# A streaming encoder layer in fp32: the first group's square moves to SBUF and GpSimd, and h comes back in one load for the final sum

## The chip, the cores and the metric

The kernel runs on one core of one Trainium2 chip. The metric is the device time of one execution in microseconds (us), as the median of several runs. The engines are called PE (TensorE), DVE (VectorE), ACT (ScalarE), POOL (GpSimd) and SP (SyncE, which issues most of the DMAs).

## What is computed

One layer of an encoder is computed in fp32 for 1024 prompt frames and 32 sample frames (whose 512 past frames lie in a cache). The model's width is 1024, the width of the feed-forward part (FFN) 4096. Two attention mixers and two gates come first; what matters here is the end of the layer:

```python
def merge_and_ffn(x, o_a, o_b, gate_a, gate_b, w_branch_a, w_branch_b, w_out, g_ffn, w_up, w_down):
    B, L = x.shape[:2]
    pa = jnp.einsum('blc,cd->bld', o_a.reshape(B, L, WIDTH_A), w_branch_a)
    pb = jnp.einsum('blc,cd->bld', o_b.reshape(B, L, WIDTH_B), w_branch_b)
    m = jax.nn.sigmoid(gate_a) * pa + jax.nn.sigmoid(gate_b) * pb
    h = x + jnp.einsum('bld,de->ble', m, w_out)
    u = jnp.einsum('bld,df->blf', rmsnorm(h, g_ffn), w_up)
    return h + jnp.einsum('blf,fd->bld', jnp.square(jax.nn.relu(u)), w_down)
```

`rmsnorm(h, g)` is h * rsqrt(mean(h^2) + eps) * g. Its factor per frame is the same for all features, so the kernel takes it out: the FFN runs on h * g, and because the square doubles the power, its result is multiplied at the end by `rb2` = 1 / (mean(h^2) + eps).

## The kernel before

**Layout and products.** Activations lie feature-major: 128 features on the partitions, frames along the free axis. Every fp32 product is made of three passes in the faster format fp32r. Each operand is split into a rounded high part and the rest, and `three` adds high x high, high x rest and rest x high into one PSUM bank. In the rows, `wh` and `wl` are the parts of a weight, `xh` and `xl` those of an activation. `unit` (L435) brings a weight of 128x512 on chip: SP loads it into `wst` (3 buffers), ScalarE casts it to `wh`, GpSimd subtracts to get `wl` (5 buffers each). So each weight that PE multiplies costs GpSimd one subtraction.

**Banks.** `column_block` (L474) takes a PSUM bank (`bank`, L426), issues the matmuls of one output tile and then calls `done`, which reads the bank. The bank is free for another tile when the last instruction that reads or writes it has ended.

**Order.** The kernel's instructions are first recorded, then put in order by a planner (`Plan`) that simulates the engines with estimated costs. Where several instructions could go next on an engine, a rank decides: FAST, then PREP (loads and weight splits), MAIN, FILL (matmuls of a column block), SLOW. Nothing is reordered on the chip: each engine runs its list in order and waits on semaphores. Since the planner issues everything, every row of the profile has the same line, L410 (`fn(*args, **kw)`), and groups are told apart by tile names.

**The two groups.** After the attention of the first frames, the end of the layer (gates, `w_out`, FFN) runs for two groups of columns. Group 0 has columns 0 to 511 in one chunk of 512. It runs beside the attention that is still left (generators called by `beside`), and attention holds six of the eight banks: the group has two, tagged `pj`. Its h * g lies in `g.h` and `g.l`, which are the tiles xh[0] and xl[0] (xh_92 and xl_93 in the rows); the squares lie in `g.mh` and `g.ml`, in xh[1] and xl[1] (xh_94, xl_95). Group 1 has columns 512 to 1055 in two chunks of 272, tiles gh and gl of its own, and all banks: six `pj` for the up-projection, two `pd` for the down-projection. Its up-projection makes two by two blocks of outputs with seven products in place of eight (`go_up_quad`), whose weight sums are formed by loads that add in flight. `hv`, the sum h of the layer's middle, is also written to DRAM (`dh`), because g.h holds it only multiplied by g and rounded.

**The FFN** (`ffn_group`, L1436). d_ff is cut in eight quarters of 512, as the code calls them. In group 0, `go_up(f)` (L1453) makes 128 features of u with 24 matmuls and two weights, and hands the bank to `square` (L1427): ScalarE writes relu to an SBUF tile `ru`, VectorE multiplies the bank by it in place (`scalar_tensor_tensor`, pj<-pj,ru in the rows), ScalarE casts the bank to `uh`, VectorE subtracts to get `ul` (the row `xl<-pj,xh`). The bank is held through all four. In group 1 the same function squares the quad's outputs, one of each pair with sign -1.

`go_down(e, q)` (L1506) multiplies the four feature blocks of quarter q with the weight for output block e (12 matmuls a chunk) and adds the bank to `g.y`: in quarter 0 ScalarE copies it, later VectorE adds, and in the last quarter VectorE multiplies the bank by rb2, adds y and SP stores the sum. So that this sum is already h + rb2 * (all others), the kernel in quarter 6 (nq - 2), behind each down-projection, loads h of this block from `dh` into a tile `hx` (tag sg, 3 buffers), and GpSimd multiplies y by rb2 and adds hx.

Per quarter, group 0 runs four up-projections (the first of them ahead of the quarter), then eight down-projections; in the last quarter two down-projections of quarter 6 (KEEP, e = 6 and 7) come between. Group 1 alternates a quad of the next quarter with four down-projections of this one. `rb2` is `g.acc`, and appears as acc in the rows.

Of the kernel before, what the change touches and what calls it, by code (L numbers as in the profile page):

```python
# [9 lines left out]
F32 = mybir.dt.float32  # L10
# [10 lines left out]
KB = D // 128  # L21
# [31 lines left out]
FAST, PREP, MAIN, FILL, SLOW = 0, 1, 2, 3, 4  # L53
# [365 lines left out]
class Layer:  # L419
# [1007 lines left out]
    def square(self, g, ps, uh, ul, sign=1.0):  # L1427

        nc = self.nc
        r = g.tmp("ru", "pb", 3)  # L1430
        nc.scalar.activation(r, ps, AF.Relu, scale=sign)
        nc.vector.scalar_tensor_tensor(ps, ps, sign, r, op0=ALU.mult, op1=ALU.mult)
        nc.scalar.copy(uh, ps)
        nc.vector.tensor_sub(ul, ps, uh.bitcast(F32))

    def ffn_group(self, g, late=iter(())):  # L1436
        nc, a, i = self.nc, self.a, g.i
        n = g.n
        rb2 = g.acc

        def scales():

            for c in range(len(g.chunks)):
                ps = self.bank("pj")
                nc.tensor.matmul(ps[:, :n], self.ones, g.acc[c], start=True, stop=True)
                with nc.rank(FAST):
                    v = g.tmp("rv", "pb", 3)
                    nc.vector.tensor_scalar(v, ps[:, :n], 1.0 / D, EPS, op0=ALU.mult, op1=ALU.add)
                    nc.vector.reciprocal(rb2[c], v)

        nq, us = DFF // 512, {}

        def go_up(f):  # L1453
            units = [self.unit(a["w_up"][f, j]) for j in range(2)]
            us[f] = uh, ul = g.mh[:, f % 8], g.ml[:, f % 8]
            self.column_block(units, lambda k, cs: (g.h[:, k, cs], g.l[:, k, cs]),
                              lambda c, cs, ps: self.square(g, ps, uh[:, cs], ul[:, cs]), g.chunks)

        def go_up_quad(f):

            a11, a12, a22, s1, s2, s3, s4 = self.quad_units(f)
            for i in range(2):
                us[f + i] = g.mh[:, (f + i) % 8], g.ml[:, (f + i) % 8]
            ta, tb, tc, td = ([(th[:, k], tl[:, k]) for k in range(4)] for th, tl in g.sums)
            x = lambda j, c: [(g.h[:, 4 * j + k, c * n:c * n + n], g.l[:, 4 * j + k, c * n:c * n + n]) for k in range(4)]

            def product(w, xs, ps=None):
                first = ps is None
                if first:
                    ps = self.bank("pj")[:, :n]  # L1470
                with nc.rank(FILL):
                    for k in range(4):
                        ks = slice(k * 128, k * 128 + 128)
                        self.three(ps, w[0][:, ks], w[1][:, ks], *xs[k], first and k == 0, k == 3, skip_group_check=True)
                return ps

            def keep(ps):
                t = nc.tile(self.op, [128, g.w], F32, "part", tag="o32", bufs=4)[:, :n]
                with nc.rank(FAST):
                    nc.scalar.copy(t, ps)  # L1480
                return t

            def done(i, c, out, ps, more=None):
                cs = slice(c * n, c * n + n)
                uh, ul = us[f + i]
                with nc.rank(FAST):
                    if more is not None:
                        nc.vector.tensor_add(out, ps, more)
                    self.square(g, out, uh[:, cs], ul[:, cs], -1.0 if i else 1.0)

            px = product(a11, x(0, 0))
            p1 = keep(px)
            pz = product(s1, ta)
            p5 = keep(pz)
            product(s2, tb, px)
            u2 = keep(px)
            product(s4, x(1, 1), pz)
            done(0, 1, pz, pz, u2)
            py = product(a12, x(1, 0))
            done(0, 0, py, py, p1)  # L1500
            product(s3, tc, px)
            done(1, 1, self.bank("pj")[:, :n], px, p5)
            product(a22, td, px)
            done(1, 0, px, px)

        def go_down(e, q):  # L1506
            units = [self.unit(a["w_down"][e, q])]

            def done(c, cs, ps):
                y = g.y[:, e, cs]  # L1510
                if q == 0:
                    nc.scalar.copy(y, ps)
                elif q < nq - 1:
                    nc.vector.tensor_add(y, ps, y)
                else:
                    nc.vector.tensor_mul(ps, ps, rb2[c])
                    nc.vector.tensor_add(y, ps, y)
                    nc.sync.dma_start(self.o["yT"][:, e, slice(g.lo + cs.start, g.lo + cs.stop)], y)

            self.column_block(units, lambda k, cs: (us[4 * q + k][0][:, cs], us[4 * q + k][1][:, cs]), done, g.chunks,  # L1520
                              kn=4, tag="pd" if g.i else "pj")
            if q == nq - 2:
                for c, cs in enumerate(g.chunks):
                    y = g.y[:, e, cs]
                    with nc.rank(PREP):
                        hx = nc.tile(self.op, [128, g.w], F32, "hx", tag="sg", bufs=3)[:, :n]
                        nc.sync.dma_start(hx, self.dh[e, :, slice(g.lo + cs.start, g.lo + cs.stop)])
                        nc.gpsimd.tensor_mul(y, y, rb2[c])
                        nc.gpsimd.tensor_add(y, y, hx)

        done = 0

        def beside(n):

            nonlocal done
            done += n
            while done >= PACE:
                done -= PACE
                nc.patience = WAIT[2]
                with nc.behind():  # L1540
                    next(late, None)
                nc.patience = WAIT[1]

        if g.i:
            go_up_quad(0)
            scales()
            go_up_quad(2)
            for q in range(nq):
                for i in range(2):
                    if q < nq - 1:  # L1550
                        go_up_quad(4 * q + 4 + 2 * i)
                    for e in range(4 * i, 4 * i + 4):
                        go_down(e, q)
            return
        go_up(0)
        scales()
        for q in range(nq):
            for f in range(4 * q + 1, min(4 * q + 5, 4 * nq)):
                go_up(f)
                beside(2)  # L1560
            if q == nq - 1:
                for e in KEEP:
                    go_down(e, q - 1)
            for e in range(KB):
                if q != nq - 2 or e not in KEEP:
                    go_down(e, q)
                beside(1)
# [81 lines left out]
```

## Time and profile before

| | |
|---|---|
| median of three runs | 1787.98 us (1787.19 to 1790.59) |
| profiled execution | 1787.43 us, its span 1785.7 us |
| mean granted TensorE clock | 0.998 of full speed |
| instructions | 32620, of them 11394 matmuls |
| traffic of the span | 264.5 MB, 148 GB/s on average |

Six stretches of the span, as busy us of each engine (the windows view):

| us of the span | what runs | PE | DVE | ACT | POOL | DMA share |
|---|---|---|---|---|---|---|
| 0 to 460 (460 us) | input projections, first attention | 450.3 | 353.8 | 296.2 | 179.9 | 0.46 |
| 460 to 850 (390) | attention, gates and w_out of group 0 | 383.2 | 253.0 | 243.5 | 278.4 | 0.63 |
| 850 to 1127 (277) | FFN of group 0 beside late attention | 272.1 | 162.2 | 156.7 | 136.2 | 0.42 |
| 1127 to 1310 (183) | FFN of group 0 alone | 179.0 | 51.1 | 63.8 | 113.9 | 0.44 |
| 1310 to 1430 (120) | gates and w_out of group 1 | 115.6 | 82.0 | 66.7 | 99.8 | 0.74 |
| 1430 to 1786 (356) | FFN of group 1 | 346.5 | 147.6 | 150.8 | 218.8 | 0.61 |

A row of the profile reads: line, engine, operation, output tile <- input tiles, partitions x elements and type. A group has a count (x32), its busy us, the mean ns of one, and behind the second bar the idle time that lay ahead of its instructions on that engine with what ended most of it. A timeline row has the start in us, the duration, the instruction, and in brackets the idle time just ahead of it and who ended it.

### The profile page before, as it was taken

Reading aid. Unit: us, or ns where it says so; the run is one execution under the profiler, and the core shown is the slowest. Engines: PE = TensorE matmul, PEld = TensorE weight load, DVE = VectorE, ACT = ScalarE, POOL = GpSimd, SP = SyncE. Lnnn points to the kernel's source line nnn. Section 1 sums busy time; section 2 is a strip of 40 time slices with the busy share of each in tenths; the row PEclk is TensorE's granted clock in tenths of the full one; section 3 lists DMA queues with packets and bytes.
Section 4 is the critical chain, followed back from the end, with each engine's and each line's share of the span. In section 5 each row is a group of like instructions: output and inputs, shape, how many; then the busy total and the mean of one; then the engine's idle time right before and its main releaser. Section 6 shows DMA issues by size and latency. Waiting matters only on the chain.

```text
span 1785.7 us, 32620 instructions
## 1 busy us (share of the span) xinstructions
PE 1746.7 (98%) x11394; PEld 1601.3 (90%) x11394; DVE 1049.7 (59%) x2304; ACT 977.7 (55%) x2153; POOL 1026.9 (58%) x901
## 2 busy tenths in 40 slices
PE   8999999999999999999999999999999999999998
PEld 7999999999899888988888888888799999999998
DVE  7555678999566645888755555222247843444434
ACT  7444599973256766666665456533236654444441
POOL 3623332435276675998664444644859966666675
PEclk9999999999999999999999999999999999999999
DMA  7244451544665667566344443533487676666633
GB/s 258 71 130 121 116 172 58 161 144 132 201 174 158 169 199 209 169 177 180 104 139 114 123 139 101 155 94 95 130 256 197 162 172 151 152 151 154 153 78 108
DMA packets 171283, 264.53 MB, mean 148 GB/s; under 512 B 29296, under 2 KB 60624, under 8 KB 171120
## 3 DMA queue, kind: packets, MB, share of 16 engines
q1 hardware_dynamic: 161472, 245.33, 47.4%
q0 software_dynamic: 9216, 16.78, 6.0%
q8 instruction: 90, 1.47, 0.3%
q14 instruction: 73, 0.60, 0.1%
q10 hardware_dynamic: 432, 0.34, 0.1%
HBM read 207.87 MB, written 54.40 MB: 147 GB/s over the span
## 4 chain that ended last, share of the span: by engine, by line
PE 83%; DMA 5%; POOL 4%; DVE 4%; issue 2%; ACT 1%; SPq 0%; ACTq 0%; POOLq 0%; DVEq 0%
PE pj L410 51%; PE s L410 13%; PE pd L410 10%; PE t L410 5%; PE o L410 4%; POOL wl L410 2%; DMA sg<-dg 1%; DVE xl L410 1%; DMA raw<-w_up 1%; POOL y L410 1%; DMA q<-dq 1%; POOL xl L410 1%; POOL acc L410 1%; POOL pb L410 0%; SPq L410 0%
## 5 line engine op out<-in xcount | busy, mean ns | idle before, releaser
L410 POOL TENSOR_TENSOR wl<-wst,wh 128x512 fp32r<-128x512 f32 x350 | 483.4, 1389 | 390.4 <-ACT wh L410 365.4
L410 PE MATMUL pj<-xh,wh 128*128 128x512 f32 (+1 forms) x1600 | 558.3, 350 | 7.0 <-DVE y L410 4.0
L410 PE MATMUL pj<-xh,wl 128*128 128x512 f32 (+1 forms) x1600 | 558.2, 350 | 0.7 <-POOL wl L410 0.7
L410 PE MATMUL pj<-xl,wh 128*128 128x512 f32 (+1 forms) x1600 | 556.6, 348 | 0.1
L410 ACT CAST wh<-wst 128x512 fp32r<-128x512 f32 x350 | 216.4, 620 | 328.8 <-PE pj L410 181.1
L410 PEld LDWEIGHTS pj<-xh,wh 128*128 128x128 f32 x1600 | 301.0, 188 | 43.5 <-DVE y L410 5.2
L410 PEld LDWEIGHTS pj<-xh,wl 128*128 128x128 f32 x1600 | 301.1, 188 | 34.2 <-POOL wl L410 1.2
L410 PEld LDWEIGHTS pj<-xl,wh 128*128 128x128 f32 x1600 | 301.3, 188 | 32.3 <-DVE xl L410 0.6
L410 PE MATMUL pd<-xh,wl 128*128 128x272 f32 x512 | 148.0, 290 | 3.3 <-POOL wl L410 3.3
L410 PE MATMUL pd<-xh,wh 128*128 128x272 f32 x512 | 148.1, 289 | 1.9 <-ACT y L410 1.6
L410 PE MATMUL pd<-xl,wh 128*128 128x272 f32 x512 | 148.0, 289 | 0.0
L410 DVE TENSOR_TENSOR tt<-t,tt 128x512 fp32r<-128x512 f32 (+2 forms) x168 | 100.3, 622 | 49.4 <-ACT tt L410 47.5
L410 DVE TENSOR_TENSOR_SCAN rem<-rem 128x896 f32<-128x896 f32 (+6 forms) x66 | 121.6, 1865 | 12.3 <-ACT rem L410 12.1
L410 ACT ACTIVATE junk<-score,cand 128x384 bf16<-128x384 f32 (+1 forms) x124 | 116.0, 936 | 9.4 <-DVE cand L410 7.3
L410 POOL TENSOR_TENSOR p<-p,rem 128x895 f32<-128x895 f32 (+6 forms) x66 | 99.2, 1516 | 32.2 <-DVE rem L410 29.8
L410 ACT CAST tt<-t 128x512 fp32r<-128x512 f32 (+2 forms) x168 | 84.7, 541 | 44.3 <-PE t L410 40.3
L410 PEld LDWEIGHTS o<-tt,v 128*128 128x128 f32 x640 | 92.6, 188 | 11.3 <-ACT wh L410 1.5
L410 PE MATMUL s<-wl,xh 128*128 128x256 f32 (+1 forms) x360 | 101.8, 286 | 0.2 <-POOL wl L410 0.2
L410 PE MATMUL s<-wh,xh 128*128 128x256 f32 (+1 forms) x360 | 100.3, 286 | 0.9 <-DVE small L410 0.7
L410 PE MATMUL s<-k,q 128*128 128x384 f32 (+5 forms) x384 | 95.7, 357 | 5.4 <-DMA k<-dk 2.3
L410 PE MATMUL s<-wh,xl 128*128 128x256 f32 (+1 forms) x360 | 100.8, 283 | 0.0
L410 PE MATMUL o<-tt,v 128*128 128x256 f32 (+1 forms) x640 | 99.0, 278 | 1.4 <-DVE o L410 0.7
(252 smaller groups left out, 3829.0 us busy)
## 6 DMA issues: line engine op xcount, KB each, us to landing
wst<-w_down SPq DMA_DIRECT2D x128, 256.0 KB, 2.7
raw<-w_up SPq DMA_DIRECT2D x80, 256.0 KB, 3.1
q<-dq SPq DMA_DIRECT2D x64, 256.0 KB, 5.3
wst<-w_up SPq DMA_DIRECT2D x64, 256.0 KB, 2.7
raw<-w_up POOLq DMA_DIRECT2D x64, 256.0 KB, 4.5
k<-dk SPq DMA_DIRECT2D x48, 256.0 KB, 3.9
v<-dv SPq DMA_DIRECT2D x48, 256.0 KB, 3.9
wst<-w_g SPq DMA_DIRECT2D x42, 256.0 KB, 3.4
```

What stands on the lines that cost most here:

```text
L410: fn(*args, **kw)
```

## The change

Two parts of the FFN are written in another way.

*The square of group 0.* The relu goes to the SBUF tile `ru` as before. GpSimd then squares that tile in place, ScalarE casts it to `uh`, and VectorE subtracts `uh` from it. The bank is read by the relu alone. Group 1's square stays as it is.

*The final sum, in both groups.* The `hx` tiles and their loads (8 in group 0, 16 in group 1) are gone. When the last up-projection is through, nothing reads `g.h` any more, and one DMA (`reload`, ranked PREP) brings all of h from `dh` into it: 128x8x512 fp32 in group 0, 128x8x544 in group 1. The sum of a block is made in two ways, in the last quarter. For e from 4 to 7 GpSimd multiplies y by rb2 and adds h, now recorded just ahead of the block's last matmuls (rank MAIN instead of PREP); VectorE then does as before. For e from 0 to 3 GpSimd does nothing: VectorE adds y to the bank, multiplies the bank by rb2 and writes bank + h to y. Each block is stored as before.

```diff
--- before.py
+++ after.py
@@ -1429,6 +1429,11 @@
         nc = self.nc
         r = g.tmp("ru", "pb", 3)
         nc.scalar.activation(r, ps, AF.Relu, scale=sign)
+        if not g.i:
+            nc.gpsimd.tensor_mul(r, r, r)
+            nc.scalar.copy(uh, r)
+            nc.vector.tensor_sub(ul, r, uh.bitcast(F32))
+            return
         nc.vector.scalar_tensor_tensor(ps, ps, sign, r, op0=ALU.mult, op1=ALU.mult)
         nc.scalar.copy(uh, ps)
         nc.vector.tensor_sub(ul, ps, uh.bitcast(F32))
@@ -1510,23 +1515,33 @@
                 y = g.y[:, e, cs]
                 if q == 0:
                     nc.scalar.copy(y, ps)
-                elif q < nq - 1:
+                    return
+                if q < nq - 1:
                     nc.vector.tensor_add(y, ps, y)
-                else:
-                    nc.vector.tensor_mul(ps, ps, rb2[c])
-                    nc.vector.tensor_add(y, ps, y)
-                    nc.sync.dma_start(self.o["yT"][:, e, slice(g.lo + cs.start, g.lo + cs.stop)], y)
-
+                    return
+                if e < KB // 2:
+                    nc.vector.tensor_add(ps, ps, y)
+                    y = hx_of(e, cs)
+                nc.vector.tensor_mul(ps, ps, rb2[c])
+                nc.vector.tensor_add(g.y[:, e, cs], ps, y)
+                nc.sync.dma_start(self.o["yT"][:, e, slice(g.lo + cs.start, g.lo + cs.stop)], g.y[:, e, cs])
+
+            if q == nq - 1 and e >= KB // 2:
+                for c, cs in enumerate(g.chunks):
+                    y = g.y[:, e, cs]
+                    nc.gpsimd.tensor_mul(y, y, rb2[c])
+                    nc.gpsimd.tensor_add(y, y, hx_of(e, cs))
             self.column_block(units, lambda k, cs: (us[4 * q + k][0][:, cs], us[4 * q + k][1][:, cs]), done, g.chunks,
                               kn=4, tag="pd" if g.i else "pj")
-            if q == nq - 2:
-                for c, cs in enumerate(g.chunks):
-                    y = g.y[:, e, cs]
-                    with nc.rank(PREP):
-                        hx = nc.tile(self.op, [128, g.w], F32, "hx", tag="sg", bufs=3)[:, :n]
-                        nc.sync.dma_start(hx, self.dh[e, :, slice(g.lo + cs.start, g.lo + cs.stop)])
-                        nc.gpsimd.tensor_mul(y, y, rb2[c])
-                        nc.gpsimd.tensor_add(y, y, hx)
+
+        def hx_of(e, cs):
+
+            return g.h.bitcast(F32)[:, e, cs]
+
+        def reload():
+
+            with nc.rank(PREP):
+                nc.sync.dma_start(g.h.bitcast(F32), self.dh[:, :, g.lo:g.lo + g.w].rearrange("e p t -> p e t"))
 
         done = 0
 
@@ -1546,6 +1561,8 @@
             scales()
             go_up_quad(2)
             for q in range(nq):
+                if q == nq - 1:
+                    reload()
                 for i in range(2):
                     if q < nq - 1:
                         go_up_quad(4 * q + 4 + 2 * i)
@@ -1559,6 +1576,7 @@
                 go_up(f)
                 beside(2)
             if q == nq - 1:
+                reload()
                 for e in KEEP:
                     go_down(e, q - 1)
             for e in range(KB):
```

## The prediction

> **What bounds the kernel now.** I read the page first.
>
> ```profile
> span 1785.7 us, 32620 instructions
> PE 1746.7 (98%) x11394; PEld 1601.3 (90%) x11394; DVE 1049.7 (59%) x2304; ACT 977.7 (55%) x2153; POOL 1026.9 (58%) x901
> ```
>
> TensorE is busy for 98% of the span, and the change neither adds nor removes a matmul. All that it can win is in the 39 us in which PE stands still, so the next view is the table of who PE waited for, cut to 740 to 1300 us, where the first group's FFN runs.
>
> ```profile
> PE pj L410 <- DVE y L410: 4.0, 5, 0.9
> PE pj L410 <- ACT y L410: 1.7, 1, 1.7
> ...
> PE pj L410 <- DVE xl L410: 0.8, 2, 0.6
> PE pj L410 <- POOL wl L410: 0.7, 1, 0.7
> ```
>
> The columns are total us, times and longest. Five waits of 0.8 us that look alike come once per quarter of the FFN, so one of them is followed in the timeline (start, duration, engine, operation; in brackets the idle time before it).
>
> ```profile
> 1244.90 0.59 ACT L410 ACTIVATE ru<-pj 128x512 f32<-128x512 f32 x1
> 1245.52 0.70 DVE L410 SCALAR_TENSOR_TENSOR pj<-pj,ru 128x512 f32<-128x512 f32 x1 [3.40 <-ACT ru L410]
> 1246.25 0.59 ACT L410 CAST xh<-pj 128x512 fp32r<-128x512 f32 x1 [0.77 <-DVE pj L410]
> 1246.85 0.39 PE L410 MATMUL pj<-xh,wl 128*128 128x512 f32 x1
> 1247.27 0.69 DVE L410 TENSOR_TENSOR y<-pj,y 128x512 f32<-128x512 f32 x1 [1.05 <-PE pj L410]
> 1247.88 0.68 DVE L410 TENSOR_TENSOR xl<-pj,xh 128x512 fp32r<-128x512 f32 x1
> 1248.02 0.50 PE L410 MATMUL pj<-xh,wh 128*128 128x512 f32 x1 [0.78 <-DVE y L410]
> 1248.36 0.40 PE L410 MATMUL pj<-xl,wh 128*128 128x512 f32 x1
> ```
>
> The group has two PSUM banks. The last up-projection of the quarter holds one from its relu at 1244.90 until `xl` ends at 1248.56. The first down-projection fills the other bank in 2.7 us and hands it back only when `y` ends at 1247.96. PE has nowhere to write in between. The price is more than the 0.78 us named: from the start at 1246.85 to that at 1248.36 pass 1.51 us, and two matmuls take 0.46 us by this row of the chain that ended last (start, us, 192 matmuls: 0.228 us each).
>
> ```profile
> 1158.81 43.85 PE pj L410 x192
> ```
>
> So a gap costs 1.05 us, the idle time and 0.27 us more. The other large stall is near the end. First VectorE, then PE, then GpSimd, and last a table of two windows (us, busy time of PE, PEld, DVE, ACT, POOL, granted clock, DMA share, GB/s).
>
> ```profile
> 1750.58 0.44 DVE L410 TENSOR_TENSOR y<-pd,y 128x272 f32<-128x272 f32 x1 [1.07 <-PE pd L410]
> 1752.08 0.44 DVE L410 TENSOR_TENSOR y<-pd,y 128x272 f32<-128x272 f32 x1 [1.06 <-PE pd L410]
> 1759.09 0.45 DVE L410 TENSOR_TENSOR pd<-pd,acc 128x272 f32<-128x272 f32 x1 [6.57 <-PE pd L410]
> 1759.64 0.44 DVE L410 TENSOR_TENSOR y<-pd,y 128x272 f32<-128x272 f32 x1
> 1760.70 0.45 DVE L410 TENSOR_TENSOR pd<-pd,acc 128x272 f32<-128x272 f32 x1 [0.61 <-PE pd L410]
> ```
> ```profile
> 1756.42 0.60 PE L410 MATMUL pd<-xh,wl 128*128 128x272 f32 x1 [3.33 <-POOL wl L410]
> ...
> 1757.04 0.43 PE L410 MATMUL pd<-xl,wh 128*128 128x272 f32 x1
> 1757.27 0.43 PE L410 MATMUL pd<-xh,wl 128*128 128x272 f32 x1
> ```
> ```profile
> 1743.05 1.29 POOL L410 TENSOR_TENSOR wl<-wst,wh 128x512 fp32r<-128x512 f32 x1
> ...
> 1754.39 0.76 POOL L410 TENSOR_TENSOR y<-y,hx 128x272 f32<-128x272 f32 x1
> 1755.10 1.26 POOL L410 TENSOR_TENSOR wl<-wst,wh 128x512 fp32r<-128x512 f32 x1
> ```
> ```profile
> 1750.00:1762.00 12.00, 8.39 (x53) 7.95 (x52) 2.67 (x6) 1.24 (x2) 10.54 (x13) 0.86 0.31 84
> 1744.00:1752.00 8.00, 8.00 (x66) 8.00 (x65) 2.21 (x5) 0.67 (x2) 7.64 (x11) 1.00 0.36 104
> ```
>
> GpSimd splits no weight between 1744.3 and 1755.1; it is busy with the `y` work of the final sum. PE stands for 3.33 us and then starts slowly: 0.23 us from matmul to matmul where 0.125 is usual (twelve in the 1.50 us between the first two VectorE rows), with the mean granted clock at 0.86. From 1752.08 to 1760.70 PE does two chunks, worth 3.0 us, in 8.62 us: this place costs 5.6 us.
>
> **The change, part by part.** *The square.* On PE, at the end of the quarter above, stands in the kernel before (pj_8338 is the up-projection's bank, 8343, 8348 and 8353 are those of down-projections 0, 1 and 2):
>
> ```order
> L410 MATMUL pj_8338<-xh0_92,wl_8337 128x512
> L410 MATMUL pj_8343<-xh1_94,wh_8341 128x512
> ...
> L410 MATMUL pj_8343<-xh1_94,wl_8342 128x512
> L410 MATMUL pj_8353<-xh1_94,wh_8351 128x512
> L410 MATMUL pj_8353<-xl1_95,wh_8351 128x512
> L410 MATMUL pj_8353<-xh1_94,wl_8352 128x512
> L410 MATMUL pj_8348<-xh1_94,wh_8346 128x512
> ```
>
> and now (8347 and 8351 are projections 1 and 2):
>
> ```order
> L410 MATMUL pj_8338<-xh0_92,wl_8337 128x512
> L410 MATMUL pj_8343<-xh1_94,wh_8341 128x512
> ...
> L410 MATMUL pj_8343<-xh1_94,wl_8342 128x512
> L410 MATMUL pj_8347<-xh1_94,wh_8345 128x512
> ...
> L410 MATMUL pj_8347<-xh1_94,wl_8346 128x512
> L410 MATMUL pj_8351<-xh1_94,wh_8349 128x512
> ```
>
> Projection 1 moves up to its turn, because its bank is free once the relu has read it. The relu took 0.59 us from 1244.90 and projection 0 ends 2.7 us after the up-projection, so nothing is late next: all seven waits named after `y` and `xl` go, 4.0 + 0.8 + 7 x 0.27 = 6.7 us. The wait after ScalarE's `y` (1.7 + 0.27 = 2.0 us) is the same place in the first quarter, but there ScalarE itself writes `y`, now behind a cast that waits for GpSimd; between 0 and 2.0 I take 1.0 gained.
>
> What is added:
>
> ```profile
> L410 POOL TENSOR_TENSOR y<-y,acc 128x512 f32<-128x512 f32 x8 | 10.2, 1291 | 1.7 <-DVE y L410 1.7
> L410 DVE TENSOR_TENSOR xl<-pj,xh 128x512 fp32r<-128x512 f32 x32 | 21.9, 685 | 14.6 <-ACT xh L410 14.6
> L410 DVE TENSOR_TENSOR xl<-pb,xh 128x512 fp32r<-128x512 f32 x8 | 12.1, 1515 | 1.9 <-ACT xh L410 1.9
> 850.00:1127.00 277.00, 272.10 (x1511) 235.29 (x1510) 162.15 (x357) 156.71 (x300) 136.24 (x105) 1.00 0.42 118
> ```
>
> 32 multiplies of 1.29 us are 41 us on GpSimd, and 32 VectorE operations of 0.7 us (22 us) go. The rest of the square gets `xl` with both inputs in SBUF, 1.5 us by the third row instead of 0.69 (27 us at most). This covers itself: beside the late attention (850 to 1127 us) GpSimd is busy 136 of 277 us, and nobody reads a square for 7.5 us (24 matmuls of the next up-projection and nine of projection 0), while relu, multiply, cast and `xl` need 0.59 + 1.29 + 0.59 + 1.5 = 4.0 us. But the multiplies stand ahead of weights and of attention probabilities on GpSimd, and the cast ahead of attention's work on ScalarE. The nearest wait of that kind:
>
> ```profile
> 808.72 0.87 PE L410 MATMUL t<-ident,p 128*128 128x128 f32 x6 [0.84 <-POOL p L410]
> ```
>
> One such wait per ten multiplies makes 2.7 us; none makes 0, one per multiply on the 20 squares of that stretch 17. I take 2.7, since half of GpSimd is free there.
>
> *The final sum, second group.* On GpSimd, behind the last up-projection weights, stand before:
>
> ```order
> L410 TENSOR_TENSOR wl<-wst,wh 128x512 x3
> L410 TENSOR_TENSOR y_14412<-y_14412,acc_14413 128x272
> L410 TENSOR_TENSOR wl<-wst,wh 128x512
> L410 TENSOR_TENSOR y_14412<-y_14412,hx 128x272
> ...
> L410 TENSOR_TENSOR y_14412<-y_14412,hx 128x272
> L410 TENSOR_TENSOR wl<-wst,wh 128x512
> L410 TENSOR_TENSOR y_14412<-y_14412,hx 128x272
> L410 TENSOR_TENSOR wl<-wst,wh 128x512 x7
> ```
>
> and now (gh holds the reloaded h):
>
> ```order
> L410 TENSOR_TENSOR wl<-wst,wh 128x512 x5
> L410 TENSOR_TENSOR y_14401<-y_14401,acc_14402 128x272
> L410 TENSOR_TENSOR wl<-wst,wh 128x512
> L410 TENSOR_TENSOR y_14401<-y_14401,acc_14403 128x272
> L410 TENSOR_TENSOR y_14401<-y_14401,acc_14402 128x272
> L410 TENSOR_TENSOR y_14401<-y_14401,gh_14399 128x272 x2
> L410 TENSOR_TENSOR wl<-wst,wh 128x512 x2
> ```
>
> The weight that PE waited for at 1756 now stands ahead of all `y` work, and 16 of the 32 `y` operations are gone from GpSimd. The 5.6 us go. VectorE's three chained operations for e below 4 take 0.55 + 0.55 + 0.44 = 1.54 us of a bank against 1.50 per chunk: up to 0.2 us on each of eight chunks with the handover, 0 to 1.6; I take 0.3, as VectorE overlaps neighbouring chunks. Net 5.3 gained. In the first group the same order frees the `wl` wait (0.7 + 0.27 = 1.0; bounds 0 and 1.0). The end is unchanged: for e = 7 a multiply, an add and a store follow the last matmul, as before.
>
> *The reload.* One load of 2 MB (2.2 in the second group) replaces 8 or 16 small ones. No load of this size is in the trace; KB each and median us to landing of the nearest, and the window in which the queues moved most:
>
> ```profile
> hx<-dh SPq DMA_DIRECT2D x8, 256.0 KB, 2.8
> xt<-x SPq DMA_DIRECT2D x8, 512.0 KB, 5.5
> out_v_b<-vt SPq DMA_DIRECT2D x4, 528.0 KB, 3.4
> 1325.00:1350.00 25.00, 23.53 (x185) 23.10 (x185) 13.35 (x21) 12.16 (x23) 16.53 (x18) 1.00 0.95 269
> ```
>
> With the slope from the first row to the third 2 MB land in 6.8 us, to the second in 21.7. At 269 GB/s they take 7.8 us, and 1.9 more is fixed (2.8 less 256 KB at that rate): 9.7, nearest to the third row, and 0.9 for a weight load ahead in the queue. In the first group the load may go when the last up-projection ends; PE then has three down-projections (8.2 us) and VectorE two operations (1.6) before h is read, and with the second bank PE stops only past 10.2 us. Estimate 10.6, cost 0.5 (0 to 13). [...] Behind the load on SP stand only weights that are wanted over 8 us later. In the second group h is wanted some 16 us after the release, so the load is hidden.
>
> **Sum.** 6.7 + 1.0 + 1.0 + 5.3 gained, 2.7 + 0.5 lost: 10.8 us less. The profiled execution took 1787.43 us (span 1785.7), 0.55 under the median of 1787.98; on the median that is **1777.2 us**.
>
> **The rivals.** *Given back at the hand-over* (0.18): the first group's gain only lets PE arrive earlier at the second group's loads; at 1325 to 1350 us DMA is 0.95 busy and PE already idles 1.5 us. Against it: those loads start earlier too. Only the tail remains: 1787.98 - 5.3 = 1782.7.
>
> *The waits come back under another name* (0.11): on GpSimd a multiply queues behind three weight splits (3.9 us), the square comes after 7.9 us instead of 4.0, past the 7.5 allowed, and the final `y` adds wait for the reload with weights behind them. Then 14.0 us gained are lost again: about 1788. For it: GpSimd is in order; against: half of its time is free.
>
> [...]
>
> *A late reload* (0.03, slower): at 21.7 us, 11.5 us lost in the first group and some 5 in the second, with slow starts of 1.4 us behind each: 19 against 14, 1793; it decides from 19 us of landing time on.
>
> **Chances.** My forecast has 0.62. About 0.2% (3.6 us) is what a measurement of this kernel can tell from no change. Faster: 0.62 + 0.18 = 0.80; same 0.11; slower 0.09. The range goes from 1772.5 (no waits added, ScalarE's wait gone too, a little over) to 1785.5, which takes in the first rival; 0.2 is left out.
>
> **What would show it.** Right: in the first FFN no PE wait after `y` or `xl` of the square; no gap over 1 us in the last 40 us, granted clock 1.00 there; the reload landing in 8 to 11 us. Wrong: new PE waits after POOL `p`, POOL `wl`, or DMA of h; `xl` beyond 2 us; PE idle growing between 1310 and 1400 us.

## The result, and the profile after

The changed kernel takes 1770.42 us (median of four runs, 1769.13 to 1771.30), the kernel before 1787.59 us beside it (four runs, 1787.09 to 1790.59). The ratio is 0.990, with a 95% interval of 0.9883 to 0.9917. That is 17.2 us less. Forecast were 1777.2 us, 10.8 less, with a range from 1772.5 to 1785.5: the direction was right, and the gain came out larger than the range allows.

The page of the changed kernel, first its span and its engines:

```profile
span 1769.5 us, 32605 instructions
PE 1741.2 (98%) x11394; PEld 1599.9 (90%) x11394; DVE 1050.6 (59%) x2284; ACT 976.5 (55%) x2153; POOL 1046.0 (59%) x909
```

The span is 16.1 us shorter. PE has the same 11394 matmuls; it now idles for 28.3 us, not 39, and its busy time, which holds the slow matmuls, is 5.5 us shorter.

Who PE waited for in the first group's FFN, in the changed kernel, from 740 to 1290 us (columns as in the prediction: us in total, times, longest):

```profile
PE t L410 <- POOL p L410: 0.8, 1, 0.8
PE o L410 <- ACT wh L410: 0.4, 1, 0.4
PE pj L410 <- ACT xh L410: 0.3, 1, 0.3
```

All three lie before 850 us. From 850 to 1290 us the same view names no wait at all. Three rows of the kernel before, which the prediction did not show, belong to the stretch from 850 us on:

```profile
PE o L410 <- DVE o L410: 0.7, 1, 0.7
PE s L410 <- issue: 0.5, 1, 0.5
PE o L410 <- ACT wh L410: 0.3, 1, 0.3
```

The end of a quarter in the timeline of the changed kernel (the place of 1244.90 in the kernel before; other rows left out):

```profile
1234.30 0.59 ACT L410 ACTIVATE ru<-pj 128x512 f32<-128x512 f32 x1
...
1235.77 1.04 POOL L410 TENSOR_TENSOR ru<-ru 128x512 f32<-128x512 f32 x1
...
1236.47 0.39 PE L410 MATMUL pj<-xh,wh 128*128 128x512 f32 x1
1236.67 0.69 DVE L410 TENSOR_TENSOR y<-pj,y 128x512 f32<-128x512 f32 x1 [3.03 <-PE pj L410]
...
1237.02 0.61 ACT L410 CAST xh<-ru 128x512 fp32r<-128x512 f32 x1
...
1237.66 1.42 DVE L410 TENSOR_TENSOR xl<-ru,xh 128x512 fp32r<-128x512 f32 x1 [0.30 <-ACT xh L410]
```

The up-projection's bank is free at 1234.89. The first down-projection fills the other one until 1236.7, and PE goes on in the free one from matmul to matmul, though the square is not finished before 1239.08. Before, PE had to wait here for `y`.

The tail, in the changed kernel's timeline of VectorE and PE:

```profile
1752.90 0.44 DVE L410 TENSOR_TENSOR y<-pd,gh 128x272 f32<-128x272 f32 x1
1753.43 0.45 DVE L410 TENSOR_TENSOR pd<-pd,y 128x272 f32<-128x272 f32 x1
1753.92 0.45 DVE L410 TENSOR_TENSOR pd<-pd,acc 128x272 f32<-128x272 f32 x1
1754.40 0.44 DVE L410 TENSOR_TENSOR y<-pd,gh 128x272 f32<-128x272 f32 x1
```
```profile
1753.11 0.29 PE L410 MATMUL pd<-xh,wl 128*128 128x272 f32 x1
1753.49 0.36 PE L410 MATMUL pd<-xh,wh 128*128 128x272 f32 x1
1753.69 0.29 PE L410 MATMUL pd<-xl,wh 128*128 128x272 f32 x1
1753.82 0.28 PE L410 MATMUL pd<-xh,wl 128*128 128x272 f32 x1
```

The stop of 3.33 us is gone. What is left is a small one for each of the blocks that VectorE sums alone: from 1753.11 to 1753.69 pass 0.58 us where two matmuls take 0.25, so 0.33 us, about four times.

The two reloads (KB, us from issue to landing):

```profile
gh<-dh SPq DMA_DIRECT2D x1, 2176.0 KB, 8.4
xh<-dh SPq DMA_DIRECT2D x1, 2048.0 KB, 8.4
```

Both traces hold the same number of matmuls, so the start of the n-th matmul can be set against that of the n-th in the other. This gives the gain of each stretch, in us (times are those of the kernel before):

| stretch | predicted | measured |
|---|---|---|
| start to 856 us; the same instructions, in the same order on the compute engines up to 854 us | 0 | 1.4 |
| FFN of group 0, to 1298 | 5.5 | 12.5 |
| hand-over and start of group 1's FFN, to 1463 | 0 | -2.3 |
| rest of that FFN, to 1752 | 0 | 0.0 |
| tail | 5.3 | 4.4 |

### The profile page after: what moved, and what is told of

Same layout as the page of the kernel before. It is cut to its first block, busy times and chain, and to the rows that moved or that the text cites. A ratio compares the mean times of both kernels' runs of the same rounds, so it can differ in the third digit from the quotient of the medians.

```text
span 1769.5 us, 32605 instructions
## 1 busy us (share of the span) xinstructions
PE 1741.2 (98%) x11394; PEld 1599.9 (90%) x11394; DVE 1050.6 (59%) x2284; ACT 976.5 (55%) x2153; POOL 1046.0 (59%) x909
## 4 chain that ended last, share of the span: by engine, by line
PE 85%; DMA 4%; POOL 4%; DVE 3%; issue 2%; ACT 1%; SPq 1%; ACTq 0%; POOLq 0%; DVEq 0%
PE pj L410 52%; PE s L410 13%; PE pd L410 11%; PE t L410 5%; PE o L410 5%; POOL wl L410 1%; DMA wst<-w_ba 1%; SPq L410 1%; DVE xl L410 1%; POOL xl L410 1%; POOL pb L410 1%; POOL acc L410 0%; DMA raw<-w_up 0%; DMA wst<-w_g 0%; DMA xt<-x 0%
## 5 line engine op out<-in xcount | busy, mean ns | idle before, releaser
L410 POOL TENSOR_TENSOR p<-p,rem 128x895 f32<-128x895 f32 (+6 forms) x66 | 100.9, 1541 | 30.3 <-DVE rem L410 25.3
L410 PEld LDWEIGHTS pd<-xh,wh 128*128 128x128 f32 x512 | 96.5, 189 | 3.3 <-ACT y L410 2.0
```

## The experiments

Theory: a PSUM bank that is given back by the relu removes all stops of PE in the first group's FFN, and the order of GpSimd's work removes the stop in the tail. Rivals: the moved engine work or the new order makes the gain; the multiplies on GpSimd cost something; the parts only work together. The table has the median, the ratio to the kernel before on the same chip with its 95% interval, and the gain against the trace of before in three of the stretches above.

| kernel | us | ratio | FFN 0 | hand-over | tail |
|---|---|---|---|---|---|
| the change | 1770.42 | 0.9883 to 0.9917 | 12.5 | -2.3 | 4.4 |
| square_alone | 1779.13 | 0.9933 to 0.9965 | 9.4 | -0.5 | -0.5 |
| sum_alone | 1782.70 | 0.9960 to 0.9987 | 1.7 | -0.8 | 4.4 |
| square_vector | 1770.72 | 0.9884 to 0.9915 | 11.4 | -1.3 | 4.4 |
| bank_held | 1794.58 | 1.0026 to 1.0059 | -12.8 | 1.5 | 4.4 |
| square_twice | 1773.06 | 0.9901 to 0.9950 | 9.9 | 0.4 | 4.4 |
| sum_gpsimd | 1770.31 | 0.9890 to 0.9945 | 10.6 | 1.1 | 5.6 |
| sum_alternate | 1767.89 | 0.9874 to 0.9920 | 12.4 | 1.0 | 4.3 |
| tail_banks | 1769.09 | 0.9875 to 0.9932 | 12.5 | -0.8 | 5.6 |
| reload_twice | 1782.60 | 0.9957 to 0.9986 | 3.7 | -0.2 | 3.0 |
| alternate_banks | 1766.99 | 0.9868 to 0.9905 | 12.4 | 2.3 | 5.6 |
| alternate_banks_q0 | 1766.78 | 0.9864 to 0.9919 | 12.5 | 0.2 | 5.6 |

**One part alone: square_alone and sum_alone.** The kernel before with the new `square` only:

```diff
         nc.scalar.activation(r, ps, AF.Relu, scale=sign)
+        if not g.i:
+            nc.gpsimd.tensor_mul(r, r, r)
+            nc.scalar.copy(uh, r)
+            nc.vector.tensor_sub(ul, r, uh.bitcast(F32))
+            return
```

> The kernel before with the new square of the first group alone; the final sum stays. Theory (the bank is given back by the relu, so every wait of PE in the first group's FFN goes, and the multiplies on GpSimd cost PE nothing): before, PE stood 13 times there, 8.85 us in all, and each stop cost 0.27 us more; less the one after wl, which belongs to the final sum, 12 stops and 8.1 + 12 x 0.27 = 11.4 us less, minus up to 2.3 us given back at the hand-over to the second group: 1776 to 1779 us, no PE stop over 0.1 us between 850 and 1260. Rival (the multiplies cost what the prediction put on them, 2.7 us, and the change of the final sum brought the rest): 1782 to 1784, with PE waits after POOL.

The changed kernel with these five lines taken out again:

> The change without the new square: only the reload and the new final sum. Theory: the tail gains 4.4 us and the first group's wait after wl (1.0 us) goes: 5.4 us less, about 1782.2 us; if the two parts are independent, this gain and that of the square alone add up to the whole 17.2. Rival (the parts help each other): the gains of both alone are 3 us or more short of 17.2 in sum.

The waits of PE with the square alone, from 850 to 1300 us, and then from 1440 us to the end:

```profile
PE pj L410 <- POOL wl L410: 1.4, 1, 1.4
PE s L410 <- issue: 0.9, 1, 0.9
```
```profile
PE pd L410 <- POOL wl L410: 3.5, 1, 3.5
PE pd L410 <- ACT y L410: 0.5, 1, 0.5
PE pd L410 <- DVE y L410: 0.3, 1, 0.3
```

No wait after `y`, `xl` or `o` is left in the first FFN, and the stop of the tail stands as before. The final sum alone is the mirror image: the tail gains 4.4 us and in the first FFN the old waits stay, but for the one after `wl` and the one after "issue". 1782.70 is close to the 1782.2 of the theory, and 1779.13 just above its 1776 to 1779. In the traces the parts add nearly up: 9.4 + 1.7 = 11.1 of 12.5 us in the FFN, where the square alone had 0.9 us of waits after "issue" and the old one after `wl` twice as long as before, and -0.5 + 4.4 = 3.9 of 4.4 in the tail. By the medians they don't: 8.4 + 4.8 = 13.2 us, 4.0 short of 17.2 and so beyond the 3 us that were named as the sign of the rival. But the intervals allow this difference, and the first 856 us, where all these kernels run the same instructions, differ by up to some 4 us between two profiles; so the runs neither show that the parts help each other nor rule it out.

The wait after "issue" is one for a load, though the view names none. In each of the traces that have it PE starts `s<-k,q`, a product of the late attention, within 0.1 us of the landing of the second load of q (before: landed 888.41, start 888.50; square alone: 1062.91 and 1063.00). It belongs to the attention and not to the square.

**The bank or the engine: square_vector and bank_held.** In the first the multiply moves to VectorE, in the second a dead VectorE instruction keeps the bank to the end of the square:

```diff
-            nc.gpsimd.tensor_mul(r, r, r)
+            nc.vector.tensor_mul(r, r, r)
```
```diff
             nc.vector.tensor_sub(ul, r, uh.bitcast(F32))
+            nc.vector.scalar_tensor_tensor(ps, ps, 0.0, ul.bitcast(F32), op0=ALU.mult, op1=ALU.mult)
             return
```

> The change with the multiply of the first group's square on VectorE instead of GpSimd, still from SBUF to SBUF, so the bank is still given back by the relu. Theory (the bank alone): as the change, 1769 to 1772 us, no PE stop in the first group's FFN. Rival (it is the move of work to GpSimd that helps): part of the gain is lost, 1774 or more, with PE waiting for VectorE there.

> The change with one dead VectorE instruction at the end of the square that reads and writes the bank (bank = bank x 0 x ul), so that the bank is held until the square is done. The values computed are not changed. Theory (the bank): the square's chain, now longer than before (0.6 + 1.1 + 0.6 + 1.3 + 0.7 = 4.3 us against 2.6), is waited for again: PE stops of 2 us or more once per quarter in the first group's FFN, 8 to 18 us lost against the change, 1778 to 1788. Rival (order or engines, not the bank): 1770 to 1773.

The engine doesn't matter: 1770.72 us, one wait of 1.3 us after "issue" (the load of q again) between 850 and 1300 us. The bank does: 1794.58 us, 24 us more than the change and also more than before. That VectorE has one more operation per square can't be the reason, since it has one more in square_vector too, and only the wait for q is lost there. PE's waits with the bank held, from 850 to 1310 us:

```profile
PE pj L410 <- DVE y L410: 5.1, 7, 0.9
PE pj L410 <- ACT wh L410: 4.4, 7, 1.0
PE s L410 <- issue: 3.6, 1, 3.6
PE pj L410 <- DVE pj L410: 2.9, 4, 0.9
```

The row after `DVE pj` is the dead instruction. Where `ACT wh` is named, the dead instruction ended within 0.1 us of that cast (at 1147.46 and 1147.52 for the stop that ends at 1147.61), so these rows hold the bank's release as well. The loss is larger than the 8 to 18 us expected: I had counted one stop per quarter, and PE stops after up-projections too, 18 times, for 12.4 us. With a slow start of 0.27 us behind each, as the kernel before has it at 1248.02, that makes 17.3 of the 25.3 us by which this FFN differs from the change's, by estimate. The stop of 3.6 us after "issue" is not the bank's: it ends at 877.38, and a load of q landed at 877.29. With 1.7 us for matmuls at half rate behind it, my estimate from the 3.40 us at a granted clock of 0.50 behind the change's stop at 1416.14 (last section), it makes 5.3 us more.

**What the multiplies cost: square_twice.** The changed kernel with

```diff
             nc.gpsimd.tensor_mul(r, r, r)
+            nc.gpsimd.tensor_mul(r, r, r)
```

> The change with the multiply on GpSimd made twice in place, so that the first group's FFN works on the fourth power of the relu instead of its square (another result, the same work for all engines but 32 multiplies more, 36 us, on GpSimd). Theory (the multiplies have slack beside PE's work; the 2.7 us that the prediction put on 32 of them are nothing): 1769 to 1773 us, stops of PE in the first FFN below 1 us in sum. Rival (GpSimd in order makes others late, as the prediction had it): 2.7 us or more lost, 1773 to 1790, with PE waits after POOL p or POOL wl between 850 and 1130.

1773.06 us. The waits of PE from 850 to 1300 us:

```profile
PE pj L410 <- DVE y L410: 1.6, 1, 1.6
PE s L410 <- DMA q<-dq: 0.4, 1, 0.4
```

Thirty-two more multiplies (the group `ru<-ru` is busy for 71.5 us instead of 36.2) make no wait after POOL in the attention stretch. The one of 1.6 us comes at 1281. There the last square is finished at 1276.34, where the change has it at 1271.72 (1.5 of these 4.6 us come from before this FFN); the first two down-projections that need it end close together, and PE waits until VectorE has gone through its three steps for the first of them (1278.50 to 1281.12). So slack for twice as many is there beside the attention, but not at the last square, which is waited for: this FFN gains 9.9 us and not 12.5. The time alone can't tell the theory (to 1773) from the rival (from 1773); that no wait after `p` or `wl` appears speaks against the rival. The expectation's sum "below 1 us" was missed.

**The tail: sum_gpsimd, sum_alternate, tail_banks.**

```diff
-                if e < KB // 2:
+                if e < 0:
...
-            if q == nq - 1 and e >= KB // 2:
+            if q == nq - 1 and e >= 0:
```

> The change with the final sum of all eight blocks prepared on GpSimd (multiply and add for e from 0 to 3 too), so that no bank waits for three chained VectorE operations. Theory (the order cures the tail, and the four stops that remain there, 1.3 us, are the price of the VectorE chain): these four stops go, and 16 more GpSimd operations of 0.77 us in some 20 us before the end stand before the last weights; if they hide, 1769; if they don't, PE waits for wl again, 1770 to 1776. Rival (the halving is what cures the tail): the stop of 3 us and the half-rate matmuls of the kernel before come back, 1774 to 1776.

In sum_alternate the two conditions are `e % 2 == 0` and `e % 2`.

> The change with the blocks e = 0, 2, 4, 6 on VectorE's chain of three and 1, 3, 5, 7 on GpSimd. Theory (a pair of chunks costs VectorE 3.3 us where PE makes it in 3.0, and VectorE can catch up in the next block, which costs it 2.1): the four stops of 0.3 us in the tail go, 1.0 to 1.3 us less than the change, 1769.2. Rival (the stops come from the bank of each chunk, not from VectorE's total): they stay in the blocks 0, 2, 4, 6 and the time is the change's.

```diff
-                              kn=4, tag="pd" if g.i else "pj")
+                              kn=4, tag="pd" if g.i and q < nq - 1 else "pj")
```

> The change with the last quarter's down-projections of the second group in the six banks of the up-projection instead of the two of their own. Theory (the four stops are waits for a bank): they go, 1.2 us less than the change, about 1769.2 us, no PE stop in the last 40 us. Rival (something else paces PE there, a weight or GpSimd's y): no stop after y, but one elsewhere, and the change's time.

With all 32 operations on GpSimd, as many as before, no PE wait is left in the tail, which gains 5.6 us: the order, with `y` block by block between the weights, is what cures it, not the halving. Up to the last weight no more than 2.9 us of `y` work now stands between two splits; before, it was 10.8 us (1744.3 to 1755.1). In the first group it has a price: PE stops for 1.4 us at 1280 (sum_gpsimd, waits from 1250 to 1300 us):

```profile
PE pj L410 <- DVE y L410: 1.4, 1, 1.4
```

It is the order on VectorE that makes it. h had landed at 1275.62, and GpSimd begins its `y` + h for the first block at 1276.54; but VectorE's next instruction is the second block's multiply (1278.68), and only then comes the first block's last addition (1279.29), which gives the bank back. So the halving avoids this stop in the first group; whether all of the work on GpSimd must have it or this plan alone, one run doesn't show. By turns, the small stops stay (three gaps of 0.09 us after VectorE's `y`, some 0.3 us each with the slow start), and the tail gains 4.3 us: the rival is right there, each block pays for its own chain. That the time is 1767.89 us all the same, less than theory or rival said, comes from the hand-over, which gains 1.0 us in this trace where the change loses 2.3, and from the early stretch. With six banks the small stops go. The tail's whole loss was 5.6 us, and the chain on VectorE had kept 1.25 us of it.

**The reload: reload_twice.** The `dma_start` of `reload` stands there twice.

> The change with each reload issued twice into the same place; the second waits for the first and lands some 8.4 us after it. Theory (the reload of the first group was hidden with only 1 us to spare: it landed at 1275.0 and VectorE read h at 1276.2): h comes 7 to 8 us too late, PE fills its two banks and stops for about 7 us near 1280, with half-rate matmuls behind it (1.7 us): 7 to 9 us lost, 1777 to 1780. In the second group the second load still lands before h is wanted, no stop there. Rival (the load has much more slack than that): under 3 us lost, 1770 to 1773.

In the change, the load of the first group was issued and h first read by VectorE at (the load's row has the issue alone; it landed 8.4 us after it):

```profile
1266.59 0.38 SPq L410 DMA_DIRECT2D xh<-dh  x1
```
```profile
1276.22 0.69 DVE L410 TENSOR_TENSOR y<-pj,xh 128x512 f32<-128x512 f32 x1
```

In reload_twice the second load was issued at 1277.20. VectorE, then PE, from 1277 us on:

```profile
1285.04 1.29 DVE L410 TENSOR_TENSOR y<-pj,xh 128x512 f32<-128x512 f32 x2 [3.71 <-DMA xh<-dh]
```
```profile
1279.48 0.39 PE L410 MATMUL pj<-xh,wl 128*128 128x512 f32 x1
1285.79 0.79 PE L410 MATMUL pj<-xh,wh 128*128 128x512 f32 x1 [5.92 <-DVE y L410]
1286.38 0.63 PE L410 MATMUL pj<-xl,wh 128*128 128x512 f32 x1
```

h lands at 1285.02 and PE stops for 5.9 us and restarts at 0.4 to 0.6 us a matmul instead of 0.23: 8.8 us lost in this FFN (3.7 us gained instead of 12.5). In the change h was there at 1275.0, 1.2 us before it was read. The stop has the size that the prediction's rival of a late reload gives: 16.0 us from the first issue (1269.02) to the landing, less the 10.2 us that PE can go on, are 5.8. The 2.9 us behind the stop are twice the 1.4 that this rival put there without a row. At 8.4 us the load is hidden. The whole, 1782.60 us, is beyond the 1777 to 1780 expected: in the second group the second load was not quite hidden (a stop of 1.4 us in the tail), and the early stretch, which no change touched, took 2.4 us more in its trace than in the change's.

**Both gains together: alternate_banks and alternate_banks_q0.** The first joins sum_alternate and tail_banks; the second also has

```diff
+                if q == 0 and g.i:
+                    nc.vector.tensor_copy(y, ps)
+                    return
```

> The final sum by turns on VectorE (even e) and GpSimd (odd e), and the last quarter of the second group in six banks: the two variants that came out under the change, together. Theory (the variant by turns won in the hand-over between the groups, the one with six banks in the tail): both gains add, no stop in the tail, 1766.5 to 1768 us. Rival (the gain by turns was the chance of one plan): 1768 to 1770.

> The same, and in the second group's first quarter y is copied out of the bank by VectorE instead of ScalarE, whose copies stood behind casts that wait for a DMA (a PE stop of 1.8 us at 1441 in the change). Theory: this stop goes, 1 to 2 us less than without it. Rival (VectorE has split weights in its queue that wait for the same DMA): the stop comes back under VectorE's name, no gain.

1766.99 and 1766.78 us, some 3.5 us under the change; by the ratios to the kernel before (0.9887 and 0.9892 against 0.9900) only 2.3 and 1.4 us. 1.25 of that is the six banks. Of the rest a part lies at the hand-over, where PE's waits of 1.1 us after `y` and 1.2 us after `pb` are gone and others come (from 1290 to 1450 us, the change first, then alternate_banks; rows under 1 us left out):

```profile
PE pj L410 <- DVE sl L410: 2.0, 1, 2.0
PE pd L410 <- ACT y L410: 1.8, 1, 1.8
PE pj L410 <- DVE pb L410: 1.2, 1, 1.2
PE pj L410 <- DVE y L410: 1.1, 1, 1.1
...
```
```profile
PE pj L410 <- DVE sl L410: 1.5, 1, 1.5
PE pj L410 <- DVE rv L410: 1.3, 1, 1.3
...
```

The wait after ScalarE's `y` went in alternate_banks already, with another order; VectorE's copy added nothing that can be measured. What in the plan moves the hand-over stays open, and so does whether these two kernels are faster than the change at all: the intervals overlap, and 1.5 us of what the change loses at the hand-over is a half-rate stretch, where the kernel before has none behind a stop of the same length (last section).

## Why the prediction was wrong

**The bank waits: the mechanism was right, and nothing came in their place.** With the bank released by the relu, PE doesn't stop once in the first FFN. The 6.7 us for the seven waits after `y` and `xl`, priced with the slow start of 0.27 us each, fit: bank_held brings such waits back, square_vector does without GpSimd. By this price all the waits of before between 850 and 1300 us, 12 with 8.7 us, come to 8.7 + 12 x 0.27 = 11.9 us; 12.5 were gained. The slow starts also show that "All that it can win is in the 39 us" was too narrow: 5.5 of the 16.1 us came out of PE's busy time.

**The failed step was "One such wait per ten multiplies makes 2.7 us".** It measured zero, and square_twice shows that beside the attention there would have been room for twice as many. The row that I took as the nearest, a transpose waiting for GpSimd's `p`, says that such a wait exists, not that an instruction put in front makes another. The count that stood beside it in the text (half of GpSimd free, nobody reads a square for 7.5 us against a chain of 4.0) gave the right answer. In the profile the chain takes 4.8 us, from 1234.30 to 1239.08. This term alone does not carry the time out of the range: with it and the reload's 0.5 us at nothing and all of ScalarE's wait gained, the sum comes to 1773.0 us. What lies beyond are the waits of the next paragraph, and luck.

**Three waits were put at nothing without a reason.** Those after `DVE o`, "issue" and `ACT wh` in the attention stretch, 1.5 + 3 x 0.27 = 2.3 us, are not named after the square, and the prediction's sum doesn't have them. All three are gone in the change. In the first the trace shows the square in the chain: VectorE's `o` stood behind a scan of the attention and the square's multiply (873.64 to 874.31 in the kernel before), and the view of waits names only the last releaser, not what had held that one up. The one after `ACT wh` (at 865.8) has no square just ahead of it; it is gone with the square alone, in another order, and why stays open. The one after "issue" is the load of q, which meets PE or not by the plan (0.5 us before, none in the change, 0.9, 1.3 and 3.6 in three experiments).

**ScalarE's `y` in the first quarter** was taken at 1.0 of 2.0 us; all of it went. **The late reload** was taken at 0.5 us; it cost none. The landing took 8.4 us, under the 9.7 estimated for the load itself (10.6 with the load ahead of it).

**The tail: right in mechanism, the cost of the VectorE chain was mis-sized.** Not 0.3 but 1.25 us (sum_gpsimd and tail_banks, 5.6, against 4.4). I had the chain at 1.54 us against 1.50 of PE; but the bank is only given back after three operations and the handover, and each stop costs 0.33 us with its slow start (1753.11 to 1753.69). The gain was 4.4, not 5.3 us.

**The hand-over** was a rival with 0.18: it gave back 2.3 us of 12.5, not the whole. The same kernel part ranges from -2.3 to +2.3 us over the runs, so this is no fixed price either, and 1.5 of the 2.3 us are the half-rate stretch of the last section. **The early stretch** gained 1.4 us by luck: the kernel before had such a half-rate stretch at 674.3, worth 1.6 us, and the change had none there.

Put together, the gain of the profile is 12.5 - 2.3 + 4.4 + 1.4 = 16.0 us of the span's 16.1. Of the 6.4 us between the 10.8 forecast and the 17.2 measured, 3.2 are new costs that never came, and 1.0 and 2.3 old waits that went beyond the forecast. The hand-over (-2.3) and the tail (-0.9) go against that; the early stretch (1.4), 0.5 of the FFN that is in no term, and the 1.1 us by which the medians differ more than the two profiled spans make up for them. By the noise the miss is narrow: the upper end of the interval, 0.9917 of 1787.98, is 1773.1 us.

**VectorE's subtraction beside GpSimd.** 0.06 of the 0.09 for a slower kernel stood on `xl` and GpSimd's multiplies stopping each other; no run shows that they do. What the runs showed is that the subtraction with both inputs in SBUF takes longer, as its row in the changed kernel says.

```profile
L410 DVE TENSOR_TENSOR xl<-ru,xh 128x512 fp32r<-128x512 f32 x32 | 40.3, 1258 | 69.2 <-ACT xh L410 69.1
L410 POOL TENSOR_TENSOR ru<-ru 128x512 f32<-128x512 f32 x32 | 36.2, 1130 | 3.3 <-ACT ru L410 3.2
```

1258 ns against 685 from PSUM. The inputs alone don't make it longer: in the same trace 6 of the 32 took 0.67 to 0.69 us (0.68 at 1021.77), the longest 1.78. Those of 1.42 us have GpSimd splitting a weight beside them (at 1237.66 for 0.87 us, until 1238.53), not squaring; how much of their length comes from that, no run shows. PE pays nothing: it has no stop in this FFN.

## What to carry to other kernels

With few PSUM banks, let the first instruction that reads a bank be the last: copy out what the rest of the chain needs and work on it in SBUF, even where each step becomes slower (here the multiply took 1.13 us on average where it had taken 0.70, the subtraction 1.26 where it had taken 0.69, and PE stopped for neither). Look up who waits for the result before putting a price on a slower step; where the count shows slack, the price to start from is nothing, and a made-up rate of new waits only spoils the sum. Work that nobody needs soon (here `y` + h) belongs between the weights in an engine's list, block by block (in the change at most 2.9 us of it between two splits), and not in one run ahead of them (10.8 us before, and a stop of 3.33 us); where it reads a late load, the last step of its chain is the place (here the chain began at 1274.75, h landed at 1275.0 and was read at 1276.22).

## What the hardware showed beside this

**Two stops of 2.0 us, one with a half-rate stretch behind it.** The table of windows for two stops of the same 2.0 us, in the changed kernel (1416.14) and in the one before (1429.16); the eighth figure is the granted clock:

```profile
1413.40:1416.80 3.40, 1.41 (x11) 1.19 (x11) 3.04 (x4) 0.90 (x2) 2.54 (x3) 1.00 1.03 187
1416.80:1420.20 3.40, 3.40 (x17) 3.40 (x17) 0.45 (x1) 1.29 (x3) 3.00 (x3) 0.50 0.83 187
```
```profile
1425.20:1428.60 3.40, 1.98 (x16) 1.76 (x15) 3.40 (x3) 1.50 (x4) 3.35 (x3) 1.00 0.97 175
1428.60:1432.00 3.40, 2.84 (x22) 2.84 (x23) 1.32 (x3) 1.19 (x3) 2.59 (x3) 1.00 0.90 214
```

In the first, PE is idle for 1.99 of 3.40 us, and the next 3.40 us run at a granted clock of 0.50, with 17 matmuls, where the kernel before has 27 at 1.00 in the 3.40 us from 1429.20. In the second the clock stays at 1.00 behind a stop of the same length; what makes the difference, these traces don't show. The kernel before has 3.40 us at 0.50 too, from 674.30 and, behind the tail's stop of 3.33 us, from 1756.30. Set against the other trace the one at 674.3 in the kernel before cost 1.6 us, and the one at 1416.8 in the change 1.5. This is part of why the first 856 us, with the same instructions, varied by some 4 us between profiles: the kernel before had the stretch at 674.3 and the change had none there. The one at 1416.8 makes 1.5 of the 2.3 us given back.
